# A decoder trunk in one kernel: PSUM in two halves with four lasting banks, and the up projection's first weight sums made beside the attention's output tiles

## The chip, the cores and the metric

The kernel runs on one core of a Trainium2 chip. The metric is the device time of one execution in microseconds (us), the median over several runs. One run is also profiled: its trace gives the start and length of every instruction on the engines: PE (TensorE, matmuls; PEld its weight loads), DVE (VectorE), ACT (ScalarE), POOL (GpSimd) and SP (SyncE, which issues most DMAs).

## The reference

Two decoder layers on x of 1024 positions x 1024 channels, all float32. Layer 0 mixes tokens with an RG-LRU block, layer 1 with RWKV-7 time mixing; both have a cross-attention into 256 memory positions and an MLP.

```python
for i in range(DEPTH):                       # DEPTH = 2
    g = ln_gains[i]
    hn = rms_norm(x, g[0])
    t = rglru_mixer(hn, ...) if i % 2 == 0 else rwkv7_mixer(hn, ...)
    x = x + rms_norm(t, g[1])
    c = mem_cross_attention(rms_norm(x, g[2]), mem_n, c_w_q[i], c_w_kv[i], c_w_o[i])
    x = x + rms_norm(c, g[3])
    m = sqrelu_mlp(rms_norm(x, g[4]), m_w_up[i], m_w_down[i])   # 1024 -> 4096 -> 1024
    x = x + rms_norm(m, g[5])
```

## The kernel before

**Products.** Every float32 operand of a large matmul is split into a high and a low part (`split`: the cast to the high part on ACT at L203, the subtraction that leaves the low part on DVE at L204), and `mm3` multiplies high x high, high x low and low x high (L304, L305, L306). One product of 128x128 weights with 512 columns is so three matmuls.

**PSUM.** Its 16 KB in each partition are eight banks of 512 float32. `psum_layout(two, one)` closes all pools and opens new ones: `two` pairs of banks (`psum()`, 128x1024, called p) and `one` single banks (`bank()`, 128x512, called q). The layouts are (4, 0) from the start and after the scan of the rwkv, (0, 8) in both MLPs and in the scan, (2, 4) in the rest of the rwkv. Since a new layout lies over the old one, the first tile of a new pool waits for the last reader of the old tiles that lay there.

**Phases.** `fphase` makes the transposed result of a projection, one weight tile of 128 columns into one pair of banks; it takes the weight tiles two by two. The queries of the cross-attention (`c_w_q`) have eight such tiles. `tphase` makes the untransposed result, one pair for each of the eight tiles of 128 positions (48 matmuls), and hands it to `post`, which `tail` gives: a root-mean-square of the tile (`rstd`: the square with its sum on ACT at L313, then two small POOL operations at L315 and L317), the gain (L611) and the residual (L612) on DVE, a second `rstd` for the next norm, and its scaling (L619). After four tiles the half is transposed on PE, by `transpose_in` (L345, with ACT at L348 and L350 and DVE at L354) or, ahead of the MLP, by `combine_in` (L370, ACT at L371).

**Cross-attention.** `xattn` runs the queries, then eight steps (four heads x two halves) of `scores`, `flip` (transposes of the softmax, L878) and `values`, each on a pair of banks, in a staggered order, and then the output projection, a `tphase` over `c_w_o`.

**MLP.** The up projection (`cphase`) multiplies 2x2 blocks with seven products rather than eight (p1 to p7), for 16 weight tiles of 256 columns. The sums of the activations (t1 to t4) come from `combine_in`, those of the weights (s1 to s4) from `combine_w`: four POOL operations of 128x512 (L412 once and L411 three times), three casts and three subtractions. `begin(i)` takes a weight tile, opens two banks and runs the first two products; `finish(i)` calls `combine_w`; then come p5, p6, p7, p3 and p4. The first two tiles go together: both `begin` and `finish`, then the transposes of the second half (`catch_up`), then each step for both. ACT copies and DVE additions take the results out (L453, L455, L464 to L486). Results are squared and spilled to DRAM with their sums; the down projection reads them back, again with seven products, and adds its banks into SBUF (L974, L976).

**Order.** The tile framework schedules the instructions: each engine runs its own list in order, and semaphores make one wait for another. The order on each list is decided when the kernel is built, so a change in buffers can reorder rows. `take` loads weights ahead of use on SP's queue; `depth` and `ahead` say how many.

**The rwkv's scan** goes through 16 chunks of 64 positions. Each chunk takes ten single banks in turn from the pool of eight.

Of the kernel before, what the change touches and what calls it, by code (L numbers as in the profile page):

```python
# [25 lines left out]
ROOM = {"w": 2}  # L26
D = 1024
KT = 8
# [19 lines left out]
class Net:  # L48
    def __init__(self, ctx, tc, I, plan=None):
# [4 lines left out]
        self.later, self.between = [], []  # L54
        self.depth, self.ahead = 2, 3
# [11 lines left out]
        self.pstack = None  # L67
        self.psum_layout(4, 0)
# [48 lines left out]
    def psum_layout(self, two, one):  # L117

        if self.rec:
            self.pp = self.pq = Nothing()  # L120
            return
        if self.pstack is not None:
            self.pstack.close()
        self.pstack = self.ctx.enter_context(ExitStack())
        pool = lambda n, b: self.pstack.enter_context(self.tc.tile_pool(name=self.nm(n), bufs=b, space=PSUM))
        self.pp = pool("pp", two) if two else None
        self.pq = pool("pq", one) if one else None
# [4 lines left out]
    def bank(self):  # L132
        return self.pq.tile([128, 512], F32, name=self.nm("q"), tag="q")
# [149 lines left out]
    def part(self):  # L283

        return self.bank() if self.pq is not None else self.psum()[:, 0:512]

    def halves(self):

        if self.pq is not None:
            return [self.bank() for _ in range(2)]  # L290
        p = self.psum()
        return [p[:, 0:512], p[:, 512:1024]]
# [148 lines left out]
    def cphase(self, w, n, B, func, evac, ahead=2):  # L441
# [4 lines left out]

        def begin(i):
            two, first = self.take(("w", w, i))
            h, l = first
            x, z = self.part(), self.part()  # L450
# [4 lines left out]
            nc.vector.tensor_add(c0[:, a], c0[:, a], z)  # L455
            st[i] = x, c0, c1, two, first

        def finish(i):
            x, c0, c1, two, first = st[i]
            st[i] = x, [], c0, c1, self.combine_w(two, first)  # L460

        def p6(x, y, c0, c1, A):
            self.product(x, A["s2"], B["t2"], False, False)
            nc.scalar.copy(c0[:, b], x)  # L464

        def p5(x, y, c0, c1, A):
            y.append(self.part())
            self.product(y[0], A["s1"], B["t1"], True, False)
            nc.scalar.copy(c1[:, b], y[0])

        def p7(x, y, c0, c1, A):
            self.product(x, A["s3"], B["t3"], False, False)
            nc.vector.tensor_add(c1[:, b], c1[:, b], x)

        def p3(x, y, c0, c1, A):
# [3 lines left out]
        def p4(x, y, c0, c1, A):  # L479
# [17 lines left out]
        def together(two, mid=lambda: None):  # L497
# [7 lines left out]
            for step in (p5, p6, p7, p3, p4):  # L505
                for i in two:
                    step(*st[i])
# [3 lines left out]
        together(range(ahead), self.catch_up)  # L511
        for i in range(ahead, n - 2):
# [3 lines left out]
            for step in (p6, p5, p7, p3, p4):  # L516
                step(*st[i])
# [27 lines left out]
    def tphase(self, rows, z, post):  # L545
# [10 lines left out]
        for tt in range(8):  # L556
# [9 lines left out]
            post(tt, p)  # L566

# [100 lines left out]
    def rglru(self, xt, post):  # L668
# [85 lines left out]

        w = I["a_w_out"][0]
# [78 lines left out]
    def xattn(self, layer, xt, post):  # L834
# [39 lines left out]
        def flip(e):  # L874
            p = self.psum()
            for mt in range(2):
                for i in range(4):
                    nc.tensor.transpose(p[:, mt * 512 + i * 128:mt * 512 + i * 128 + 128],  # L878
                                        e[:, i * 256 + mt * 128:i * 256 + mt * 128 + 128], self.ident)
            return self.split(p)  # L880

        def values(hd, hf, pt):
            ph, pl = pt
            p = self.psum()
            for j in range(2):
                c = slice(hd * 256 + j * 128, hd * 256 + j * 128 + 128)
                for mt in range(2):
                    s = slice(mt * 512, mt * 512 + 512)
                    vh, vl = vt[mt]
                    self.mm3(p[:, j * 512:j * 512 + 512], (vh[:, c], vl[:, c]), (ph[:, s], pl[:, s]), mt == 0, mt == 1)  # L890
            nc.scalar.copy(z[hf][:, 2 * hd:2 * hd + 2, :], p.rearrange("p (j t) -> p j t", t=512))
# [11 lines left out]
        self.tphase([w[k * 128:k * 128 + 128, :] for k in range(KT)], self.tile_of(z), post)  # L903


    def mlp(self, layer, xt, raw, post, late=None):
# [30 lines left out]
        self.psum_layout(0, 8)  # L937
        rest = self.cphase(up, 16, xt, AF.Relu, out)
        self.depth, self.ahead = DOWN
# [11 lines left out]
        W = lambda g: self.take(("d", down[g * 1024:g * 1024 + 1024, :], g))  # L951
        W(0)
        for g in range(4):
# [3 lines left out]
            for n, (name, qa, qb, bank, begins, ends, to) in enumerate(steps):  # L957
                if n == 5 and g < 3:
                    W(g + 1)
                A = self.take(("a", g, qa))  # L960
                B = self.take(("b", qb, g))
                for p in range(4):
                    if begins:
                        ps[bank, p] = self.bank()
# [138 lines left out]
def rwkv(self, X, xt, lw_wa, lw_g, post):  # L1103
# [13 lines left out]
    self.psum_layout(2, 4)  # L1117
# [369 lines left out]
    def scan_gram(c, groups):  # L1487
# [3 lines left out]
        for g in groups:  # L1491
            gt = self.unit()[:, 0:768].rearrange("p (q h w) -> p q h w", q=2, h=2)
            pv = self.bank().rearrange("p (q h w) -> p q h w", q=2, h=2)
# [11 lines left out]
            if c < 15:  # L1505
                if g % 2 == 0:
                    s["tp"] = self.bank().rearrange("p (q h i) -> p q h i", q=4, h=2)
# [33 lines left out]
    def flip_out(c):  # L1541
        s = cst.pop(c)
        y, (g1, g2) = s["y"], s["gs"]
        p = self.part()
# [23 lines left out]
    self.psum_layout(0, 8)  # L1568
    for h in range(2):
        nc.gpsimd.memset(cst[0]["sv"][hr[h], :, h, :], 0.0)  # L1570
    for c in range(16):
# [10 lines left out]
        yp = self.bank()  # L1582
        Y = yp.rearrange("p (q i) -> p q i", i=64)
        for m in range(2):
            ph = self.bank()
# [46 lines left out]
    self.psum_layout(4, 0)  # L1632
# [10 lines left out]
def network(net, I, out):  # L1643
# [12 lines left out]
    for l in range(2):  # L1656
# [5 lines left out]
        net.xattn(l, nxt, post)  # L1662
# [27 lines left out]
```

## Time and profile before

| | us |
|---|---|
| median of 3 runs | 3017.53 (3016.5 to 3020.7) |
| profiled execution, its own time | 3011.39 |
| its span in the trace | 3009.7 |
| PE busy | 2867.0 |
| DVE busy | 1811.5 |
| ACT busy | 1357.9 |
| POOL busy | 1152.8 |

A busy time is the sum of an engine's instructions; engines run beside each other, so the five don't add up to the span. The views quoted below are: the page (shares of the span), the waits of an engine (for whom it stood idle, how long in total, how often, and the longest), windows (busy times in one stretch of the span, with the clock that TensorE was granted, 1.00 being full speed), and the timeline (start, length, engine, line, operation, tiles out<-in, shape, count; in brackets the idle time before it and what ended that).

### The profile page before, as it was taken

How to read it: one execution, taken by the hardware profiler on the slowest of the kernel's cores; microseconds unless marked ns; L12 is line 12 of the kernel's file. 1: busy time of each engine (PE TensorE's matmuls, PEld its weight loads, DVE VectorE, ACT ScalarE, POOL GpSimd, SP SyncE). 2: the span in 40 equal slices, each digit the busy share in tenths (PEclk: the TensorE clock that was granted, in tenths of full speed). 3: DMA queues.
4: the chain of work that ended last, by engine and by line, in shares of the span. 5: the costliest groups of instructions: out<-in, count | busy, mean ns of one | idle time of the engine just before them, and what ended most of it. 6: DMA issues, size and time to landing. Idle time of an engine off the chain costs nothing. (4 is left out here: it accounts for less than half of the span.)

```text
span 3009.7 us, 42878 instructions
## 1 busy us (share of the span) xinstructions
PE 2867.0 (95%) x16987; PEld 2382.3 (79%) x16987; DVE 1811.5 (60%) x1996; ACT 1357.9 (45%) x1943; POOL 1152.8 (38%) x1055
## 2 busy tenths in 40 slices
PE   7999999898999999989999899989999899999998
PEld 6888798786888878877877578878888688887886
DVE  5576552547345688867785536884354744568776
ACT  6464342535455543347442534442243545454332
POOL 2000100015666664431486225651001556667442
PEclk9999999998999999999999999999999999999999
DMA  8213261122444564332656889852312244455443
GB/s 258 73 46 94 88 210 60 57 84 70 153 154 152 213 225 146 119 116 89 183 155 183 220 246 228 175 127 96 100 50 77 84 140 154 154 210 203 158 136 119
DMA packets 382889, 421.93 MB, mean 140 GB/s; under 512 B 91248, under 2 KB 293216, under 8 KB 382688
## 3 DMA queue, kind: packets, MB, share of 16 engines
q1 hardware_dynamic: 370656, 379.19, 42.0%
q0 software_dynamic: 11568, 39.41, 3.5%
q8 instruction: 134, 2.20, 0.3%
q14 instruction: 67, 0.55, 0.1%
q10 hardware_dynamic: 464, 0.59, 0.1%
HBM read 284.31 MB, written 134.74 MB: 139 GB/s over the span
## 5 line engine op out<-in xcount | busy, mean ns | idle before, releaser
L204 DVE TENSOR_TENSOR u<-u,u 128x1024 fp32r<-128x1024 f32 (+1 forms) x518 | 818.6, 1608 | 355.3 <-ACT u L203 335.3
L304 PE MATMUL p<-u,u 128*128 128x512 f32 (+1 forms) x1920 | 716.7, 376 | 18.2 <-ACT u L203 9.5
L203 ACT CAST u<-u 128x1024 fp32r<-128x1024 f32 (+1 forms) x550 | 542.7, 1024 | 421.4 <-PE q L305 158.7
L305 PE MATMUL p<-u,u 128*128 128x512 f32 (+1 forms) x1920 | 718.1, 374 | 9.4 <-DVE u L204 9.4
L306 PE MATMUL p<-u,u 128*128 128x512 f32 (+1 forms) x1920 | 714.9, 373 | 3.8 <-DVE u L204 3.7
L304 PE MATMUL q<-u,u 128*128 128x512 f32 (+1 forms) x1632 | 642.5, 395 | 25.2 <-ACT u L203 8.3
L305 PE MATMUL q<-u,u 128*128 128x512 f32 (+1 forms) x1632 | 638.5, 392 | 7.0 <-DVE u L204 7.0
L306 PE MATMUL q<-u,u 128*128 128x512 f32 (+1 forms) x1632 | 633.6, 391 | 0.0
L304 PEld LDWEIGHTS p<-u,u 128*128 128x128 f32 x1920 | 366.5, 191 | 84.5 <-ACT u L203 13.5
L305 PEld LDWEIGHTS p<-u,u 128*128 128x128 f32 x1920 | 367.6, 191 | 74.5 <-DVE u L204 14.6
L306 PEld LDWEIGHTS p<-u,u 128*128 128x128 f32 x1920 | 367.2, 191 | 67.4 <-DVE u L204 5.8
L315 POOL TENSOR_SCALAR s<-s 128x1 f32<-128x1 f32 x98 | 36.1, 369 | 992.2 <-ACT u L313 991.2
L304 PEld LDWEIGHTS q<-u,u 128*128 128x128 f32 (+1 forms) x1632 | 308.3, 190 | 97.0 <-ACT u L203 13.5
L305 PEld LDWEIGHTS q<-u,u 128*128 128x128 f32 (+1 forms) x1632 | 308.8, 189 | 73.0 <-DVE u L204 9.3
L306 PEld LDWEIGHTS q<-u,u 128*128 128x128 f32 (+1 forms) x1632 | 308.3, 189 | 64.4
L431 POOL TENSOR_TENSOR u<-u,u 128x1024 f32<-128x1024 f32 x64 | 179.2, 2823 | 86.5 <-DVE u L204 80.4
L976 DVE TENSOR_TENSOR z<-z,q 128x512 f32<-128x512 f32 x192 | 128.9, 681 | 90.4 <-PE q L306 90.2
L204 POOL TENSOR_TENSOR u<-u,u 128x1024 fp32r<-128x1024 f32 x32 | 95.0, 2968 | 164.0 <-ACT u L203 101.9
L411 POOL TENSOR_TENSOR u<-u,u 128x512 f32<-128x512 f32 x96 | 150.8, 1580 | 2.9
L927 POOL TENSOR_TENSOR u<-u,u 128x512 f32<-128x512 f32 x32 | 47.1, 1471 | 166.2 <-ACT u L916 160.1
L304 PE MATMUL q<-z,u 128*128 128x512 f32 x256 | 102.1, 399 | 7.0 <-DVE u L611 7.0
L611 DVE SCALAR_TENSOR_TENSOR u<-p,s,u 128x1024 f32<-128x1024 f32 x24 | 30.8, 1284 | 122.1 <-ACT u L203 77.9
(260 smaller groups left out, 3536.5 us busy)
## 6 DMA issues: line engine op xcount, KB each, us to landing
u<-d SPq DMA_DIRECT2D x198, 512.0 KB, 4.4
d<-u SPq DMA_DIRECT2D x109, 512.0 KB, 3.5
d<-u POOLq DMA_DIRECT2D x68, 512.0 KB, 4.1
d<-u SPq DMA_DIRECT2D x132, 256.0 KB, 3.7
u<-in_m_w_up SPq DMA_DIRECT2D x64, 512.0 KB, 5.8
u<-in_m_w_down SPq DMA_DIRECT2D x64, 512.0 KB, 5.9
u<-in_c_w_kv SPq DMA_DIRECT2D x32, 512.0 KB, 6.5
u<-d SPq DMA_DIRECT2D x56, 256.0 KB, 6.1
```

Of the source, the lines that this page charges most:

```text
L203: self.nc.scalar.copy(hv, src)
L204: (eng or self.nc.vector).tensor_tensor(lv, src, hv, ALU.subtract)
L304: mm(o, ah, bh, start=first, stop=False, **kw)
L305: mm(o, ah, bl, start=False, stop=False, **kw)
L306: mm(o, al, bh, start=False, stop=last, **kw)
L315: nc.gpsimd.tensor_scalar(v, ss, 1.0 / n, eps, ALU.mult, ALU.add)
L411: sub = lambda o, x, y: nc.gpsimd.tensor_tensor(o, x, y, ALU.subtract)
L431: self.nc.gpsimd.tensor_tensor(f[o][i], f[x][i], f[y][i], ALU.subtract)
L611: nc.vector.scalar_tensor_tensor(o, src, r, gb, ALU.mult, ALU.mult)
L927: tt(s1, r21, r22, ALU.add)
L976: nc.vector.tensor_add(to_, to_, o)
```

## The change

PSUM is seen as two halves of four banks. The first, `still`, is opened once, at the first output projection (`a_w_out`), and its four single banks are kept to the end of the kernel. The other half is either two pairs ("mixed") or four more single banks ("banks"). Until `a_w_out` all eight banks are four pairs ("pairs"), as before. `bank(n)` takes pool n modulo the number of single pools.

- In the layout "mixed" (output projections, queries, cross-attention, rwkv but for its scan) there are two pairs where there were four; the transposes, the memory's keys and values, `flip` and `values` use still banks, with a split or a copy for each half.
- `fphase` takes its first two weight tiles together and each further one alone.
- `make` takes up the weight tiles 0 and 1 of the up projection, and makes their sums (`combine_w`), after tiles 5 and 6 of the attention's output projection (`MAKE`); `begin` and `finish` use what is there.
- In `cphase` the first two tiles stand in still banks (`place`), and the layout "banks" is opened after the transposes of the second half; from then on tiles alternate between the two pools.
- `then` takes up the first weights and operands of the down projection behind p7 of the last two tiles, where they were taken after the up projection.
- The scan chooses its banks by chunk, group or half.

Core of the diff:

```diff
-    def psum_layout(self, two, one):
+    def psum_layout(self, kind):
...
+        if self.stack_a is not None:
+            self.stack_a.close()
+        if kind != "pairs" and self.stack_b is None:
+            self.stack_b = self.ctx.enter_context(ExitStack())
+            self.still = pool(self.stack_b, 4)
+        self.stack_a = self.ctx.enter_context(ExitStack())
+        other = pool(self.stack_a, {"pairs": 4, "mixed": 2, "banks": 4}[kind])
+        self.pp = None if kind == "banks" else other
+        self.pqs = [] if kind == "pairs" else [self.still] if kind == "mixed" else [self.still, other]
...
+    def bank(self, n=0):
...
+        return self.pqs[n % len(self.pqs)].tile([128, 512], F32, name=self.nm("q"), tag="q")
...
+MAKE = (5, 6)
+    def make(self, w, i):
+        self.depth, self.ahead = 0, 2 - 2 * i
+        two, first = self.take(("w", w, i))
+        self.made[i] = two, first, self.combine_w(two, first)
...
+        place = lambda i: 0 if i < ahead else (i + 1) % 2
...
+            x, z = self.bank(place(i)), self.bank(place(i))
...
+                if step is p7 and two[-1] == n - 1:
+                    with self.behind():
+                        then()
...
+        def second_half():
+            self.catch_up()
+            self.psum_layout("banks")
+        together(range(ahead), second_half)
...
-        for i in range(0, len(fs), 2):
-            pair = fs[i:i + 2]
+        for pair in [fs[:2]] + [[f] for f in fs[2:]]:
...
             post(tt, p)
+            if mid:
+                mid(tt)
...
-    self.psum_layout(2, 4)
+    self.psum_layout("mixed")
...
-    self.psum_layout(0, 8)
+    self.psum_layout("banks")
...
-        net.xattn(l, nxt, post)
+        net.xattn(l, nxt, post, lambda tt: tt in MAKE and net.make(I["m_w_up"][l], MAKE.index(tt)))
```

What that does to the lists of the engines, at three places. In the rows an operation stands with its tiles out<-in; s are small tiles of statistics, u and z tiles in SBUF, p pairs and q single banks in PSUM. The lines of the new kernel are some 14 to 33 higher: L203 is L217, L313 is L327, L315 and L317 are L329 and L331, L411 and L412 are L425 and L426, L453 is L476, L304 to L306 are L318 to L320.

POOL at the end of layer 0's output projection, before: the statistics of the last tile, then the sums of weight tile 0 (u_4621 and u_4622) and the first of tile 1.

```order
L315 TENSOR_SCALAR s_5244<-s_5242 128x1
L317 TENSOR_TENSOR s_5246<-s_5244,nhalf 128x1
L315 TENSOR_SCALAR s_5255<-s_5253 128x1
L317 TENSOR_TENSOR s_5257<-s_5255,nhalf 128x1
L315 TENSOR_SCALAR s_5265<-s_5263 128x1
L317 TENSOR_TENSOR s_5267<-s_5265,nhalf 128x1
L412 TENSOR_TENSOR u_5319<-u_4622 128x512
L411 TENSOR_TENSOR u_5320<-u_4621,u_4622 128x512
L411 TENSOR_TENSOR u_5319<-u_5319,u_4621 128x512
L411 TENSOR_TENSOR u_5320<-u_4621,u_5319 128x512
L412 TENSOR_TENSOR u_5374<-u_4634 128x512
```

And in the new kernel, where u_4688 and u_4689 are weight tile 1:

```order
L329 TENSOR_SCALAR s_5252<-s_5250 128x1
L331 TENSOR_TENSOR s_5254<-s_5252,nhalf 128x1
L426 TENSOR_TENSOR u_5272<-u_4689 128x512
L425 TENSOR_TENSOR u_5273<-u_4688,u_4689 128x512
L425 TENSOR_TENSOR u_5272<-u_5272,u_4688 128x512
L329 TENSOR_SCALAR s_5263<-s_5261 128x1
L425 TENSOR_TENSOR u_5273<-u_4688,u_5272 128x512
L331 TENSOR_TENSOR s_5265<-s_5263,nhalf 128x1
L329 TENSOR_SCALAR s_5341<-s_5339 128x1
L331 TENSOR_TENSOR s_5343<-s_5341,nhalf 128x1
L329 TENSOR_SCALAR s_5352<-s_5350 128x1
L331 TENSOR_TENSOR s_5354<-s_5352,nhalf 128x1
```

The sums of weight tile 1 now stand between the statistics of the last three tiles, and those of tile 0 further ahead; behind the last statistics no weight sum is left.

ACT at the same place, before: p_5192 is the pair of the output projection's last tile, q_5289 the first bank of the up projection.

```order
L313 ACTIVATE u_5241,s_5242<-p_5192 128x1024
L313 ACTIVATE u_5173,s_5253<-u_5180 128x1024
L203 CAST u_5285<-u_4633 128x1024
L313 ACTIVATE u_5241,s_5263<-u_5248 128x1024
L453 COPY u_5291<-q_5289 128x512
L203 CAST u_5325<-u_5319 128x1024
L203 CAST u_5329<-u_5320 128x1024
L203 CAST u_5333<-u_4622 128x512
L203 CAST u_5340<-u_5281 128x1024
L453 COPY u_5346<-q_5344 128x512
L203 CAST u_5380<-u_5374 128x1024
```

And in the new kernel, where these are p_5289 and q_5374:

```order
L327 ACTIVATE u_5102,s_5261<-u_5109 128x1024
L217 CAST z_5244<-u_5226 128x1024
L217 CAST u_5278<-u_5272 128x1024
L217 CAST u_5282<-u_5273 128x1024
L217 CAST u_5286<-u_4689 128x512
L327 ACTIVATE u_5338,s_5339<-p_5289 128x1024
L476 COPY u_5376<-q_5374 128x512
L327 ACTIVATE u_5249,s_5350<-u_5256 128x1024
L327 ACTIVATE u_5338,s_5360<-u_5345 128x1024
L476 COPY u_5406<-q_5404 128x512
```

The casts of weight tile 1's sums (u_5272, u_5273 and u_4689) went from behind the first bank's copy to a place ahead of the last tile's square.

PE in layer 0's queries, before: p_3529 and p_3530 are the pairs of the first two weight tiles, p_3707 that of the third.

```order
L305 MATMUL p_3707<-u_2837,u_3519 128x512
L306 MATMUL p_3707<-u_2833,u_3520 128x512
L304 MATMUL p_3707<-u_2833,u_3519 128x512
L304 MATMUL p_3529<-u_3582,u_3445 128x512
L304 MATMUL p_3530<-u_3582,u_3475 128x512
L305 MATMUL p_3707<-u_2837,u_3519 128x512
L306 MATMUL p_3707<-u_2833,u_3520 128x512
L305 MATMUL p_3529<-u_3586,u_3445 128x512
L306 MATMUL p_3529<-u_3582,u_3446 128x512
L305 MATMUL p_3530<-u_3586,u_3475 128x512
```

And in the new kernel, where the first two are p_3540 and p_3541 and the third p_3716:

```order
L318 MATMUL p_3541<-u_3593,u_3486 128x512
L319 MATMUL p_3540<-u_3597,u_3456 128x512
L320 MATMUL p_3540<-u_3593,u_3457 128x512
L319 MATMUL p_3541<-u_3597,u_3486 128x512
L320 MATMUL p_3541<-u_3593,u_3487 128x512
L318 MATMUL p_3716<-u_2839,u_3530 128x512
L319 MATMUL p_3716<-u_2843,u_3530 128x512
L320 MATMUL p_3716<-u_2839,u_3531 128x512
```

Before, matmuls of the third tile stood among the last of the first two, in a pair that was free; now the third begins when both are through.

More of the change, by code (lines that the diff above doesn't have):

```diff
@@ L115, in small, with pool @@
         return self.sp.tile([128, 4], F32, name=self.nm("s"), tag="s")[:, :n]
-    def psum_layout(self, two, one):
+    def psum_layout(self, kind):
         if self.rec:
-            self.pp = self.pq = Nothing()
+            self.pp, self.pqs = Nothing(), []
             return
[L122 to L127, printed above, removed]
+        def pool(stack, bufs):
+            return stack.enter_context(self.tc.tile_pool(name=self.nm("pm"), bufs=bufs, space=PSUM))
+        if self.stack_a is not None:
[7 more added lines that the diff above has]
+        self.pqs = [] if kind == "pairs" else [self.still] if kind == "mixed" else [self.still, other]
     def psum(self):
         return self.pp.tile([128, 1024], F32, name=self.nm("p"), tag="p")
-    def bank(self):
-        return self.pq.tile([128, 512], F32, name=self.nm("q"), tag="q")
+    def bank(self, n=0):
+        if self.rec:
+            return Nothing()
+        return self.pqs[n % len(self.pqs)].tile([128, 512], F32, name=self.nm("q"), tag="q")
     def dram(self, shape, dt=F32):
@@ L283, in part @@
     def part(self):
-        return self.bank() if self.pq is not None else self.psum()[:, 0:512]
+        return self.bank() if self.pqs else self.psum()[:, 0:512]
     def halves(self):
-        if self.pq is not None:
-            return [self.bank() for _ in range(2)]
+        if self.pqs:
+            return [self.bank(n) for n in range(2)]
         p = self.psum()
@@ L445, in cphase @@
         st = {}
+        place = lambda i: 0 if i < ahead else (i + 1) % 2
         def begin(i):
-            two, first = self.take(("w", w, i))
+            two, first = self.made[i][:2] if i in self.made else self.take(("w", w, i))
             h, l = first
-            x, z = self.part(), self.part()
+            x, z = self.bank(place(i)), self.bank(place(i))
             c0, c1 = self.unit(), self.unit()
@@ L506, in together @@
                 for i in two:
-                    step(*st[i])
+                    step(*st[i], i)
+                if step is p7 and two[-1] == n - 1:
+                    with self.behind():
+                        then()
             for i in two:
                 end(i)
-        together(range(ahead), self.catch_up)
+        def second_half():
+            self.catch_up()
+            self.psum_layout("banks")
+        together(range(ahead), second_half)
         for i in range(ahead, n - 2):
@@ L936, in mlp, with then @@
         self.depth, self.ahead = UP
-        self.psum_layout(0, 8)
-        rest = self.cphase(up, 16, xt, AF.Relu, out)
-        self.depth, self.ahead = DOWN
+        W = lambda g: self.take(("d", down[g * 1024:g * 1024 + 1024, :], g))
+        ops = []
+        def then():
+            self.depth, self.ahead = 0, 0
+            W(0)
+            ops.extend([self.take(("a", 0, 0)), self.take(("b", "b11", 0))])
+            self.depth, self.ahead = DOWN
+        rest = self.cphase(up, 16, xt, AF.Relu, out, then)
         acc = self.big((4, 1024))
@@ L1543, in flip_out @@
         y, (g1, g2) = s["y"], s["gs"]
-        p = self.part()
+        p = self.bank(c + 1)
         for q in range(4):
```

65 lines of the change are left out of this document (32 added, 33 removed).

## The prediction

> **What bounds the kernel now.** The page first: the share of the span by engine.
>
> ```profile
> span 3009.7 us, 42878 instructions
> PE 2867.0 (95%) x16987; PEld 2382.3 (79%) x16987; DVE 1811.5 (60%) x1996; ACT 1357.9 (45%) x1943; POOL 1152.8 (38%) x1055
> ```
>
> PE is busy in 95% of the span and no other engine is over 60%. The change alters no matmul's size and adds none, so it can pay only in what PE loses: idle time between matmuls, and matmuls at a lower granted clock. Second, the windows view, for the stages that the diff touches (length, busy time of PE, PEld, DVE, ACT and POOL, granted clock, DMA share, GB/s):
>
> ```profile
> 692.70:763.20 70.50, 56.00 (x225) 44.64 (x226) 52.55 (x36) 39.42 (x52) 37.63 (x23) 0.85 0.25 73
> 2355.30:2425.80 70.50, 55.80 (x226) 44.56 (x226) 52.64 (x36) 39.42 (x52) 37.80 (x23) 0.85 0.25 74
> 760.00:1090.00 330.00, 329.06 (x1452) 271.83 (x1451) 180.90 (x132) 171.22 (x216) 224.26 (x163) 1.00 0.54 183
> 1840.00:2010.00 170.00, 158.55 (x2830) 141.87 (x2831) 141.34 (x345) 78.59 (x214) 109.46 (x132) 1.00 0.82 179
> ```
>
> The body of the first MLP (third row) has nothing to win: 1452 matmuls in 330.0 us, 0.227 us each, PE idle for 0.9 us. The starts of both MLPs (first two rows) are poor: 192 matmuls and 32 transposes take 70.5 us, of which 14.5 are idle, at a clock of 0.85. The scan (last row) has 11.5 us of idle in 170. Third, the waits view of PE (who waits, for what, us in total, times, longest):
>
> ```profile
> PE q L304 <- ACT u L203: 8.3, 4, 2.5
> PE q L304 <- DVE u L611: 7.0, 2, 3.5
> PE q L304 <- ACT z L350: 6.6, 1, 6.6
> PE q L304 <- ACT u L464: 6.1, 2, 3.0
> PE q L1625 <- DVE u L1611: 5.2, 9, 2.9
> PE q L370 <- DVE u L455: 4.7, 2, 2.4
> PE q L1589 <- DVE u L1619: 4.5, 7, 1.5
> PE q L370 <- ACT u L371: 3.4, 2, 1.8
> ```
>
> A wait of L304 on L611 is no want of data: L611 is the last reader of the output projection's last pair of banks, and the MLP's pool of eight banks opens over that pair. L350 is the same at the rwkv's entry. These two waits are what the still banks can remove.
>
> **MLP starts, two of them.** T is 692.69, where the output projection's last matmul ends. PE's rows after it:
>
> ```profile
> 696.18 0.50 PE L304 MATMUL q<-z,u 128*128 128x512 f32 x1 [3.50 <-DVE u L611]
> 713.52 0.93 PE L370 MATMUL q<-ident,u 128*128 128x128 f32 x4 [2.35 <-DVE u L455]
> 716.23 1.97 PE L370 MATMUL q<-ident,u 128*128 128x128 f32 x8 [1.79 <-ACT u L371]
> 745.45 0.79 PE L304 MATMUL q<-u,u 128*128 128x512 f32 x1 [3.04 <-ACT u L464]
> ```
>
> The 3.50 us are the wait for the last pair; the first 48 matmuls then run largely at half clock (0.50 us and more each). The 2.35 us before the transposes come from DVE, and DVE is late because of POOL. The three engines beside it:
>
> ```profile
> 692.78 1.02 ACT L313 ACTIVATE u<-p 128x1024 f32<-128x1024 f32 x1 [1.96 <-PE p L306]
> 698.02 1.06 ACT L313 ACTIVATE u<-u 128x1024 f32<-128x1024 f32 x1 [2.15 <-DVE u L612]
> 715.50 4.15 ACT L371 ACTIVATE u<-q,colt 128x512 f32<-128x512 f32 x7
> ...
> 697.84 1.22 DVE L204 TENSOR_TENSOR u<-u,u 128x1024 fp32r<-128x1024 f32 x1
> 700.12 1.76 DVE L619 TENSOR_SCALAR u<-u,s 128x1024 f32<-128x1024 f32 x1 [1.06 <-POOL s L317]
> 705.40 7.46 DVE L204 TENSOR_TENSOR u<-u,u 128x1024 fp32r<-128x1024 f32 x4 [1.07 <-ACT u L203]
> 720.61 5.30 DVE L204 TENSOR_TENSOR u<-u,u 128x1024 fp32r<-128x1024 f32 x2 [1.41 <-ACT u L203]
> 728.23 18.95 DVE L204 TENSOR_TENSOR u<-u,u 128x1024 fp32r<-128x1024 f32 x9
> ...
> 700.05 1.28 POOL L412 TENSOR_TENSOR u<-u 128x512 f32<-128x512 f32 x1
> 705.62 2.28 POOL L412 TENSOR_TENSOR u<-u 128x512 f32<-128x512 f32 x1
> 707.86 6.13 POOL L411 TENSOR_TENSOR u<-u,u 128x512 f32<-128x512 f32 x3
> ```
>
> The sums of weight tiles 0 and 1 (eight POOL operations, L411 and L412) run from T+7.4 to T+21.3, between the moment when PE could go on and the transposes. The change moves them, their six casts and six subtractions beside projection tiles 6 and 7, where each tile keeps PE busy for 48 x 0.227 = 10.9 us. New schedule, step by step:
> - The first 48 matmuls start at T, since the four still banks aren't held by the projection: 10.9 us, to T+10.9.
> - The transposes need tile 7's last operation (L619), which ends at T+9.2 now (700.12 + 1.76). In the new order of ACT the three casts of the second combination stand ahead of tile 7's statistics (some 2.6 us by the casts' usual 1.05, 1.05 and 0.5), so I take T+12: a gap of about 1 us.
> - Of the four still banks two hold the first products, so the 32 transposes run through two. A group of four takes 0.98 on PE and 0.59 on ACT (4.15 / 7); two banks give (0.98 + 0.59) / 2 = 0.79 a group, and eight groups 6.3: T+18.5 to T+19.
> - The 10 products p5 to p4 of both tiles are 120 matmuls, 27.2 us. DVE sets the pace as before: its splits of t1 took 2.65 each (5.30 / 2), the nine that follow 2.1. From the end of the transposes t1 is there after 7.7, t2 after 14.2, and from p7 on PE is behind: about 33 us with some 5.5 idle, to T+52. Now part of the third tile's first products fills these waits (PE takes them out of turn); in the new order it stands behind p4, so the holes are bare.
> - The third tile's 24 matmuls: 5.4, T+57.5. With 1 to 3.5 us for a clock that falls in those holes: T+58.5 to T+61.
>
> Against T+70.5 that is 9.5 to 12 for each MLP; I take 10.5 each, **21 in all**. The bounds: 3 each if POOL comes late (a rival below), 14 if the holes close as well.
>
> What hides the moved work: POOL, ACT and DVE beside tiles 6 and 7. The eight POOL operations cost 1.28 each alone and up to 2.28 beside DVE, so 10 to 18 us in 21.8 us of two tiles, where POOL otherwise does only the statistics. Queued behind them on POOL are just those statistics (L315, L317): for tile 6 there is a whole tile of slack, for tile 7 none. The two weight tiles are loaded long before, so SP's queue gains nothing there.
>
> How the two engines get on beside each other: a DVE split takes 1.22 alone and 7.46 / 4 = 1.87 or 5.30 / 2 = 2.65 beside POOL, a POOL sum 1.28 or 2.28. [...]
>
> **Queries (c_w_q), two of them.** Before, four pairs of banks serve weight tiles two by two, the next two free. Now there are two pairs: both are in use by the first two tiles, whose matmuls alternate and end together, so the third tile waits for an evacuation. No such wait is in the trace; the rows nearest to it:
>
> ```profile
> 536.83 1.01 ACT L203 CAST u<-p 128x1024 fp32r<-128x1024 f32 x1 [4.42 <-PE p L306]
> 537.87 1.23 DVE L204 TENSOR_TENSOR u<-p,u 128x1024 fp32r<-128x1024 f32 x1 [4.21 <-ACT u L203]
> 1571.42 0.47 PE L304 MATMUL p<-u,u 128*128 128x512 f32 x1 [1.94 <-DVE u L1354]
> 1539.65 0.64 PE L304 MATMUL p<-u,u 128*128 128x512 f32 x1 [2.79 <-DVE u L1185]
> ```
>
> Cast and subtraction of one pair take 2.3 us after its last matmul, so PE idles about 2.0; after 1.94 the next matmul still took 0.47 and after 2.79 it took 0.64, so a stretch at half clock may follow (1.7 us if 3.4 us long). Bounds 2.0 and 3.7 each, I take 2.9: **5.8 lost**. The later single tiles cover their 2.3 us with 10.9 us of matmuls.
>
> **The core of the cross-attention.** Two pairs serve the scores alone, the flips and values get single banks with a copy for each half, which frees them sooner, at two more operations for each step on ACT. I take +0.75 for each layer, **1.5** (-1 to +3).
>
> **Entry of the rwkv.**
>
> ```profile
> 1346.29 0.80 PE L304 MATMUL q<-u,u 128*128 128x512 f32 x1 [6.59 <-ACT z L350]
> 1365.19 0.75 DVE L619 TENSOR_SCALAR u<-u,s 128x1024 f32<-128x1024 f32 x1 [0.72 <-POOL s L317]
> 1370.91 1.91 PE L345 MATMUL q<-ident,u 128*128 128x128 f32 x16
> ```
>
> The 6.59 go: the still banks carry over. But the next transposes (1370.91) need L619 of the last tile, which ends at 1365.95 whatever PE does. PE saves at most 1370.91 - 1365.95 = **4.9** (0 to 9, the top if DVE moves up too); the rest turns into a wait on L619.
>
> **At nothing:** the scan's banks by number (-4 to +4; its matmuls keep their order) and the earlier first weights of the down projection (-3 to +3; layer 0's border between up and down lies inside the third row of the windows, where PE idles 0.9 us in all).
>
> **Sum:** 21 - 5.8 + 1.5 + 4.9 = 21.6. The profiled execution took 3011.4 (span 3009.7 and 1.7 around it); 21.6 less is 2989.8. The median of the runs, 3017.5, lies 6.1 over that execution, so **2996**.
>
> **The rivals.**
> - *POOL is late.* If contention stretches the eight sums past T, tile 7's statistics stand behind them, and the transposes start at T+16 and not T+12, with a stretch at half clock on top: 5 to 6 less at each MLP. With 3.7 lost at each query phase the gain is near 9: 3009. For: DVE rows that double beside POOL. Against: 21.8 us of cover. 17%.
> - *It doesn't do what it says.* The still banks are also those of the first half's transposes (L370); if these are held, the first matmuls wait as before. Gain: -5.8 + 1.5 + 4.9, about 0.6: 3017. For: four banks, eight transposes' groups. Against: those end during tile 7. 8%.
> - *The shorter waits cost no clock.* The wait of 1.94 left the next matmul at 0.47. If the waits that are left (all under 3 us) lower no clock, 0.9 at each query phase and some 2 at each MLP come back: about 6, 2990. Against: matmuls of 0.64 after 2.79 and of 0.79 after 3.04 (745.45). 10%. [...]
> - *Slower: the scan.* Its banks came from one ring of eight; now from two rings of four, chosen by chunk and group. If a chunk's bank is still read when its number comes round, PE waits there in each of 16 chunks. To turn 21.6 into a loss of 6 it takes 27.6 / 16 = 1.7 us a chunk: 3025 at 1.8 us. For: the waits L1589 and L1625 show a chain with no slack. Against: a chunk takes ten banks (one for y, two for the maps, six for the next chunk's products, one for the flip), so a ring of four comes round in most of a chunk, not in a step. 5%.
>
> **How the numbers follow.** The forecast has 60%, from 2985 to 3005. The range goes from 2979 (the MLP starts at their upper bound) to 3012 (the late POOL with its unknowns). 0.2%, 6 us, is about what a measurement can tell: faster 83% (the forecast, the clock rival, three quarters of the late POOL), within 12%, slower 5%.
>
> **What would show it.** Right: at both MLP starts the first matmul within 0.3 us of the projection's last; transposes at about T+12; 192 matmuls by T+61; no L350 wait at the rwkv but one on L619; a new wait of about 2 us in each c_w_q; the scan's row unchanged within 4 us. Wrong: projection tiles 6 and 7 over 10.9 us each, tile 7's L317 behind L411's successor after T+3, or waits on reused banks in the scan.

## The result, and the profile after

| | before | after |
|---|---|---|
| median of the runs, us | 3017.0 (4 runs) | 2990.6 (4 runs) |
| ratio after to before | | 0.9916, 95% interval 0.9904 to 0.9928 |
| span of the profiled execution, us | 3009.7 | 2990.2 |

The change makes the kernel 0.8% faster, 22 to 29 us by the interval and 19.5 us by the two profiled executions. The forecast was 2996, in a range from 2979 to 3012. The page after, the same two lines as before:

```profile
span 2990.2 us, 42725 instructions
PE 2861.3 (96%) x16987; PEld 2381.1 (80%) x16987; DVE 1812.9 (61%) x2012; ACT 1355.9 (45%) x1975; POOL 1166.1 (39%) x1055
```

PE is busy for 5.7 us less with the same number of recorded instructions (its mean granted clock is 0.983 where it was 0.980), and idle for less. The windows of the two MLP starts and of the first MLP's body after the change (length, busy time of PE, PEld, DVE, ACT, POOL, granted clock, DMA share, GB/s):

```profile
690.80:750.30 59.50, 52.64 (x226) 41.35 (x225) 41.96 (x33) 36.73 (x49) 30.59 (x20) 0.94 0.35 115
...
760.00:1075.00 315.00, 313.63 (x1379) 258.10 (x1378) 172.02 (x126) 163.40 (x208) 211.12 (x152) 1.00 0.54 181
```

The first row is the work of the row of 70.50 us before, 192 matmuls and 32 transposes: 59.5 us now, 6.9 of them idle in place of 14.5, at a clock of 0.94 in place of 0.85. PE's waits after:

```profile
PE q L318 <- DVE z L1014: 8.2, 3, 3.9
...
PE q L359 <- ACT u L1171: 4.4, 1, 4.4
...
PE q L384 <- DVE u L650: 3.5, 2, 1.7
```

The waits for L611 (7.0 us), for L350 (6.6), for L464 (6.1) and of the transposes for L455 (4.7) are gone or small. In their place stand a wait of the second half's transposes for the last tile's scaling (L650, which was L619), one at the rwkv's entry, and two long ones in the down projections (L1014, which was L976).

The span cut at points that both traces have: the first scores of each cross-attention, the end of its output projection (T), the 192nd matmul of the up projection after T, and the start of the last addition of the down projection. Times are in us.

| stretch | before | after | saved | forecast |
|---|---|---|---|---|
| start to layer 0's first scores | 538.8 | 540.9 | -2.0 | -2.9 |
| layer 0: cross-attention to T | 153.9 | 150.0 | 3.9 | 0.8 |
| layer 0: T to 192 matmuls | 70.6 | 59.5 | 11.1 | 10.5 |
| layer 0: rest of the MLP | 576.1 | 582.8 | -6.7 | 0 |
| rwkv and layer 1's queries | 863.8 | 859.2 | 4.6 | 4.9 - 2.9 |
| layer 1: cross-attention to T | 152.2 | 149.3 | 2.9 | 0.7 |
| layer 1: T to 192 matmuls | 70.6 | 60.3 | 10.3 | 10.5 |
| layer 1: rest of the MLP | 573.5 | 578.8 | -5.3 | 0 |
| the end | 10.3 | 9.5 | 0.8 | 0 |
| all | 3009.7 | 2990.2 | 19.5 | 21.6 |

The sum came out within 2.1 us, but two terms that were nearly nothing in the forecast are not: the rest of the MLPs lost 12 us, and the cross-attentions gained 5 more than forecast. The experiments take these apart.

### The profile page after: what moved, and what is told of

Same layout as the page of the kernel before. It is cut to its first block, busy times and chain, and to the rows that moved or that the text cites. A ratio compares the mean times of both kernels' runs of the same rounds, so it can differ in the third digit from the quotient of the medians.

```text
span 2990.2 us, 42725 instructions
## 1 busy us (share of the span) xinstructions
PE 2861.3 (96%) x16987; PEld 2381.1 (80%) x16987; DVE 1812.9 (61%) x2012; ACT 1355.9 (45%) x1975; POOL 1166.1 (39%) x1055
## 5 line engine op out<-in xcount | busy, mean ns | idle before, releaser
L217 ACT CAST u<-u 128x1024 fp32r<-128x1024 f32 (+1 forms) x550 | 542.8, 1023 | 372.7 <-PE q L319 139.6
L319 PE MATMUL q<-u,u 128*128 128x512 f32 (+2 forms) x1824 | 699.8, 385 | 12.4 <-DVE u L218 12.1
L318 PE MATMUL q<-u,u 128*128 128x512 f32 (+2 forms) x1824 | 696.6, 386 | 12.9 <-DVE z L1014 8.2
L320 PE MATMUL q<-u,u 128*128 128x512 f32 (+2 forms) x1824 | 694.3, 384 | 1.1 <-DVE u L218 1.1
L318 PE MATMUL p<-u,u 128*128 128x512 f32 (+1 forms) x1728 | 658.6, 384 | 22.7 <-ACT u L217 9.7
L319 PE MATMUL p<-u,u 128*128 128x512 f32 (+1 forms) x1728 | 657.1, 380 | 6.2 <-DVE u L218 6.2
L320 PE MATMUL p<-u,u 128*128 128x512 f32 (+1 forms) x1728 | 656.2, 380 | 3.5 <-DVE u L218 3.5
L329 POOL TENSOR_SCALAR s<-s 128x1 f32<-128x1 f32 x98 | 38.1, 389 | 969.0 <-ACT u L327 949.6
L318 PEld LDWEIGHTS q<-u,u 128*128 128x128 f32 (+1 forms) x1824 | 344.4, 189 | 84.7 <-DVE z L1014 8.8
L319 PEld LDWEIGHTS q<-u,u 128*128 128x128 f32 (+1 forms) x1824 | 344.7, 189 | 82.7 <-DVE u L218 16.2
L318 PEld LDWEIGHTS p<-u,u 128*128 128x128 f32 x1728 | 331.6, 192 | 87.8 <-ACT u L217 14.7
L320 PEld LDWEIGHTS q<-u,u 128*128 128x128 f32 (+1 forms) x1824 | 344.6, 189 | 69.0 <-DVE u L218 2.2
L319 PEld LDWEIGHTS p<-u,u 128*128 128x128 f32 x1728 | 331.8, 192 | 66.8 <-DVE u L218 10.5
L320 PEld LDWEIGHTS p<-u,u 128*128 128x128 f32 x1728 | 331.3, 192 | 65.7 <-DVE u L218 5.2
L1014 DVE TENSOR_TENSOR z<-z,q 128x512 f32<-128x512 f32 x192 | 129.0, 680 | 84.8 <-PE q L320 84.2
L425 POOL TENSOR_TENSOR u<-u,u 128x512 f32<-128x512 f32 x96 | 152.7, 1596 | 3.1
L320 PE MATMUL q<-z,u 128*128 128x512 f32 x256 | 99.5, 390 | 1.1 <-DVE u L218 1.1
```

Of the source, the lines that this page charges most:

```text
L217: self.nc.scalar.copy(hv, src)
L318: mm(o, ah, bh, start=first, stop=False, **kw)
L319: mm(o, ah, bl, start=False, stop=False, **kw)
L320: mm(o, al, bh, start=False, stop=last, **kw)
L329: nc.gpsimd.tensor_scalar(v, ss, 1.0 / n, eps, ALU.mult, ALU.add)
L425: sub = lambda o, x, y: nc.gpsimd.tensor_tensor(o, x, y, ALU.subtract)
```

## The experiments

Ratios are to the kernel before, run on the same chip; small effects are read from the spans of the profiled executions (2990.2 for the changed kernel) and from their stretches. Single executions of the changed kernel differ by up to 7 us, so a difference of a few us between two spans counts only where a stretch shows it too.

### What the lasting banks and the weight sums do at the MLP's start

**The lasting banks without the sums.**

```diff
-MAKE = (5, 6)
+MAKE = ()
```

> The changed kernel with no weight sums ahead of the MLP (its two tiles' sums are made at the MLP's start, as before the change); the lasting banks stay. Theory (both parts count): the first matmul still follows the output projection at once, but the transposes wait for the sums again, so each MLP start takes about 7 us more than in the changed kernel (T+66 to T+68 for its first 192 matmuls against T+59.5); 14 us over the changed kernel, about 3005. Rival (the lasting banks do it all): within 3 us of the changed kernel, about 2991.

Ratio 0.9953 (0.9940 to 0.9965), span 2996.6. PE at layer 0's start, and POOL after T = 690.8:

```profile
700.27 0.50 PE L320 MATMUL q<-z,u 128*128 128x512 f32 x1 [3.12 <-DVE u L218]
711.68 6.62 PE L384 MATMUL q<-ident,u 128*128 128x128 f32 x28 [4.54 <-DVE u L478]
...
693.94 1.28 POOL L426 TENSOR_TENSOR u<-u 128x512 f32<-128x512 f32 x1
...
704.33 5.62 POOL L425 TENSOR_TENSOR u<-u,u 128x512 f32<-128x512 f32 x3
```

The first matmul follows T at once, but the sums run from T+3.1 to T+19, tile 1's first split comes late (3.12) and most transposes start at T+20.9. The 192 matmuls end at T+63.3 and T+63.0: 3.8 and 2.7 us later than in the changed kernel, not 7. Both parts count, but the sums only for half of what I expected, since PE has the first products to do while they run.

**The sums without the lasting banks:** the kernel before with `make` and its two callers added.

```diff
-    def tphase(self, rows, z, post):
+    def tphase(self, rows, z, post, mid=None):
...
             post(tt, p)
+            if mid:
+                mid(tt)
```

> The kernel before, with its PSUM layouts, and only the weight sums moved beside output tiles 5 and 6. Theory (both parts count, and add): the first matmul waits 3.5 us for the last pair as before, the transposes no longer wait for POOL, and each MLP start is 6 to 8 us shorter: 12 to 16 under the kernel before, about 3003. Rival (the two work only together): under 4 us gained.

Ratio 0.9976 (0.9967 to 0.9985), span 3004.9. PE and POOL at layer 0's start, T = 694.6:

```profile
701.78 0.80 PE L306 MATMUL q<-z,u 128*128 128x512 f32 x1 [7.21 <-DVE u L621]
...
692.66 1.05 POOL L317 TENSOR_SCALAR s<-s 128x1 f32<-128x1 f32 x1
693.78 2.13 POOL L413 TENSOR_TENSOR u<-u,u 128x512 f32<-128x512 f32 x1
695.87 1.53 POOL L319 TENSOR_TENSOR s<-s,nhalf 128x1 f32<-128x1 f32 x1
698.61 0.23 POOL L317 TENSOR_SCALAR s<-s 128x1 f32<-128x1 f32 x1 [1.21 <-ACT u L315]
698.92 1.41 POOL L319 TENSOR_TENSOR s<-s,nhalf 128x1 f32<-128x1 f32 x1
```

The transposes start at T+20.3 and run without a wait, but the wait for the last pair (L621, L611 in the kernel before) has doubled, from 3.50 to 7.21: the casts and the last sum stand ahead of tile 7's statistics, and the eight banks of the MLP open over its pair. The 192 matmuls end at T+64.7 and T+64.5. So the four cases, in us from T (layer 0, layer 1):

| | sums at the MLP's start | sums beside the output tiles |
|---|---|---|
| PSUM as before | 70.6, 70.6 | 64.7, 64.5 |
| lasting banks | 63.3, 63.0 | 59.5, 60.3 |

The banks alone give 7.4, the sums alone 6.0, both 10.7. They don't add up fully.

**The place of the sums.**

```diff
-MAKE = (5, 6)
+MAKE = (6, 7)
```

> The changed kernel with the sums after output tiles 6 and 7 instead of 5 and 6. Theory (POOL's lateness decides, by way of tile 7's statistics): tile 1's sums stand beside tile 7's statistics after T, the transposes start some 4 us later than T+13.6, and each MLP start is 3 to 5 us longer: 6 to 10 over the changed kernel, about 2999. Rival (the cover is ample, the place of the sums does not matter): within 2 us of the changed kernel.

Ratio 0.9952 (0.9939 to 0.9966), span 2996.8: 6.6 over the changed kernel. PE at the transposes, T = 691.0:

```profile
708.38 3.52 PE L384 MATMUL q<-ident,u 128*128 128x128 f32 x16 [4.38 <-DVE u L478]
```

The transposes start at T+17.4, the 192 matmuls end at T+63.3 and T+64.1. One tile too late costs as much as leaving the sums where they were. And one tile earlier:

```diff
-MAKE = (5, 6)
+MAKE = (4, 5)
```

> The changed kernel with the sums after output tiles 4 and 5, one tile earlier. Theory (tile 7's statistics wait for POOL's last sum, which ends 3 us after T): with the sums gone by T the transposes start at about T+12 and not T+13.6, 1 to 2 us less at each MLP start, 2 to 4 under the changed kernel. Rival (the sums' six more SBUF tiles, held one tile longer, or the earlier casts and subtractions delay the output tiles): the output projection's tiles take over 10.9 us each, and the kernel is slower than the changed one.

Ratio 0.9896 (0.9880 to 0.9913), span 2980.4. The row of PE where the transposes start, T = 689.2, beside those of the changed kernel, T = 690.8:

```profile
700.90 1.09 PE L384 MATMUL q<-ident,u 128*128 128x128 f32 x8 [0.41 <-DVE u L478]
```

```profile
702.17 0.55 PE L384 MATMUL q<-ident,u 128*128 128x128 f32 x3 [0.47 <-DVE u L478]
704.46 4.00 PE L384 MATMUL q<-ident,u 128*128 128x128 f32 x17 [1.73 <-DVE u L650]
```

With the sums one tile earlier all transposes run from T+10.7 to T+16.7, and the 192 matmuls end at T+56.2 in both layers, 3.3 and 4.1 us sooner. The wait for L650 is gone. ACT shows how POOL held tile 7 up in the changed kernel: two casts of tile 1's sums, which wait for POOL's last sum, stand ahead of the square of tile 7.

```profile
693.95 1.57 ACT L217 CAST u<-u 128x1024 fp32r<-128x1024 f32 x2 [2.31 <-POOL u L425]
695.42 1.02 ACT L327 ACTIVATE u<-p 128x1024 f32<-128x1024 f32 x1
```

The square so starts at T+4.6; with the sums one tile earlier it starts at T. The rival of the late POOL was real, at 3 to 4 us an MLP rather than 5 to 6; of the 2.9 us at the transposes' start the forecast had priced 1.3 (T+12 against T+10.7).

### The start of the down projection

The first down weights and operands taken up after the up projection, as before the change:

```diff
-        rest = self.cphase(up, 16, xt, AF.Relu, out, then)
+        rest = self.cphase(up, 16, xt, AF.Relu, out, lambda: None)
+        self.depth, self.ahead = DOWN
...
+        W(0)
         for g in range(4):
```

> The changed kernel with the first down weights and operands taken up after the up projection, as before the change. Theory (taking them up early is what costs 3 to 5 us at the start of each down projection): the wait of 3.9 us at the second group of the down projection goes back to 2.5, with no stretch at half clock, 5 to 9 us under the changed kernel, about 2984. Rival 1 (the wait comes from POOL and DVE splitting the second group's operands, whenever the first is taken): within 2 us of the changed kernel. Rival 2 (the early take-up pays): over the changed kernel by 3 or more.

Ratio 0.9889 (0.9875 to 0.9902), span 2979.7. PE's wait ahead of the down projection's second group, in the changed kernel and in this one, with DVE beside it:

```profile
1091.59 0.80 PE L318 MATMUL q<-u,u 128*128 128x512 f32 x1 [3.88 <-DVE z L1014]
...
1081.26 9.68 DVE L218 TENSOR_TENSOR u<-u,u 128x1024 fp32r<-128x1024 f32 x3
1090.86 0.67 DVE L1014 TENSOR_TENSOR z<-z,q 128x512 f32<-128x512 f32 x1
```

```profile
1081.25 0.47 PE L318 MATMUL q<-u,u 128*128 128x512 f32 x1 [2.31 <-DVE z L1009]
...
1071.01 9.49 DVE L218 TENSOR_TENSOR u<-u,u 128x1024 fp32r<-128x1024 f32 x3
1080.43 0.67 DVE L1009 TENSOR_TENSOR z<-z,q 128x512 f32<-128x512 f32 x1
```

In both, three splits of 3.2 us each stand ahead of the addition that PE waits for, so the splits alone don't make the difference; what differs is their place on DVE's list: behind the eighth addition of the down projection here, behind the eleventh in the changed kernel. Without the early take-up the wait is 2.31, near the 2.46 of the kernel before, and the next matmul takes 0.47, not 0.80. The rest of the MLP takes 578.6 and 574.6 us, against 582.8 and 578.8: 4.2 us in each layer are the price of the early take-up, 1.6 of it the longer wait and most of the rest the clock (in layer 0 it was 0.50 from 1090.03 to 1096.86 in the changed kernel, and 1.00 from 1078 to 1086 in this one). All eight profiled kernels with the operands taken up early take 582.2 to 582.9 and 578.0 to 580.1 us there, the three without 577.7 to 578.6 and 574.6 to 574.7. (The other 2 us of the span saved lie in the rwkv.) The next run tells which part of it:

```diff
             W(0)
-            ops.extend([self.take(("a", 0, 0)), self.take(("b", "b11", 0))])
```

> The changed kernel in which only the first down weights are taken up beside the last up tiles, and the first operands (with their splits) after the up projection. Theory (the early splits shift the order on DVE, so that the second group's wait grows from 2.3 to 3.9 us): the wait goes back to about 2.3 and the kernel is 5 to 10 us under the changed kernel, like the one without any early take-up. Rival (the early loads of the weights shift it): the 3.9 us stay, within 3 us of the changed kernel.

Ratio 0.9883 (0.9869 to 0.9896), span 2976.4. The wait is 2.85 us, with the clock at 1.00 after it (1084.7 to 1091.5), and the rest of the MLP takes 578.6 and 574.7 us, as without any early take-up. So the loads do no harm; taking up the operands, with their splits, does. That it acts by the order on DVE is read from these rows and not shown by itself. The span is 13.8 us under the changed kernel, over the 5 to 10 that I expected: besides the 8.3 us here, 3.7 lie in layer 1's cross-attention and MLP start, which this edit doesn't reach.

### The queries, one by one

```diff
-        for pair in [fs[:2]] + [[f] for f in fs[2:]]:
+        for pair in [[f] for f in fs]:
```

> The changed kernel with all eight weight tiles of the queries taken one by one, the first two as well. Theory (two pairs that end together cost a wait of 2 us and sometimes a stretch at half clock): the wait of 1.91 us before the third tile goes, 2 to 3.6 us at each of two places, 4 to 7 under the changed kernel, about 2985. Rival (the second tile's first half covers the transposes of the input's second half): without its 24 matmuls, 5.4 us, PE waits for those transposes, up to 5 us at each place, up to 10 over the changed kernel.

Ratio 0.9860 (0.9847 to 0.9874), span 2966.7: 23.5 us under the changed kernel, far over what I expected, so the gain had to be elsewhere. Layer 0's scores begin 3.4 us earlier, and its wait of 1.91 is gone; in layer 1 the same wait stays (1.91 us, before the third tile): the first two tiles seem to take turns there all the same. Some 20 us lie in the rwkv: the wait of 11.39 us ahead of L1435 is gone, and with it 13.65 us at half clock (1673.71 to 1687.36), 4.87 of which PE was busy (from 1655 to 1668, the place in this run, its matmuls take 0.39). ACT there, in the changed kernel and in this one:

```profile
1680.36 1.04 ACT L217 CAST u<-u 128x1024 fp32r<-128x1024 f32 x1 [11.99 <-DMA u<-in_b_w_rkv]
1681.42 1.01 ACT L1425 COPY u<-p 128x1024 f32<-128x1024 f32 x1
```

```profile
1659.69 1.04 ACT L217 CAST u<-u 128x1024 fp32r<-128x1024 f32 x1
1662.30 1.02 ACT L1425 COPY u<-p 128x1024 f32<-128x1024 f32 x1 [1.57 <-PE p L320]
```

In the changed kernel a cast that waits 12 us for a weight's load stands on ACT ahead of the copy that PE waits for. With single tiles the copy doesn't stand behind such a cast. Two runs test this reading: the single tiles in the queries alone, and in the kernel before everywhere but in the queries.

```diff
-        for pair in [fs[:2]] + [[f] for f in fs[2:]]:
+        for pair in [[f] for f in fs] if len(fs) == 8 else [fs]:
```

> The changed kernel with the eight weight tiles of the queries taken one by one, but the pairs of tiles in the rwkv's projections kept. Theory (the gain of some 20 us with single tiles everywhere comes from the rwkv, where a cast that waits for a late weight stands ahead of the copy that frees PE): only the 2.9 us of layer 0's queries are gained, nothing in layer 1, and the wait of 11.4 us in the rwkv stays: 2 to 4 us under the changed kernel. Rival (the queries' order moves the rwkv's loads): most of 23 us is gained here too.

Ratio 0.9908 (0.9895 to 0.9922), span 2986.1, 4.1 under the changed kernel; the wait in the rwkv is there, 11.79 us.

```diff
-        for i in range(0, len(fs), 2):
-            pair = fs[i:i + 2]
+        n = 1 if len(fs) == 2 else 2
+        for i in range(0, len(fs), n):
+            pair = fs[i:i + n]
```

> The kernel before with only the lists of two weight tiles taken one by one (the rwkv's and the recurrent block's projections); its queries still go in pairs. Theory (the 12.4 us wait of the rwkv and its stretch at half clock come from the pairs, whatever the layout of PSUM): 15 to 22 us under the kernel before, a ratio near 0.994. Rival (it takes the new layout, with its two pairs, to gain): within 5 us of the kernel before.

Ratio 0.9940 (0.9927 to 0.9954), span 2992.4, 17.3 under the kernel before (20.0 in the rwkv itself): those 17 to 20 us can be had without the change.

### The rwkv's entry and its scan

Pools closed and opened anew at the entry, and one ring of eight banks for the scan:

```diff
-    self.psum_layout("mixed")
+    self.psum_layout("new")
```

> The changed kernel with the lasting banks closed and opened anew at the rwkv's entry. Theory (the lasting banks earn 3.8 us there): the wait of 6.6 us for the transposes' last reader is back, and the stage takes 3 to 5 us more than in the changed kernel. Rival (the wait of 4.45 us that took its place gives all of it back): within 1 us.

Ratio 0.9932 (0.9918 to 0.9946), span 2993.6. From the start of the down projection's last addition to ACT's first copy of the scan's products it takes 483.8 us, against 480.0 with the lasting banks: 3.8 us. The row of PE with new pools, and the one that stands in its place in the changed kernel:

```profile
1340.05 0.80 PE L321 MATMUL q<-u,u 128*128 128x512 f32 x1 [6.22 <-DVE u L371]
```

```profile
1360.45 5.38 PE L359 MATMUL q<-ident,u 128*128 128x128 f32 x24 [4.45 <-ACT u L1171]
```

```diff
-    self.psum_layout("banks")
+    self.psum_layout("ring")
```

> The changed kernel with one ring of eight banks in the rwkv's scan, as before the change, in place of two pools of four chosen by chunk and group. Theory (the split of the banks costs nothing): the scan's 16 chunks take the same time within 2 us. Rival: the two pools cost or earn over 3 us in the scan.

Ratio 0.9921 (0.9908 to 0.9934), span 2989.4: no difference that can be told. Within the rwkv the ring reaches that first copy 5.2 us earlier and takes 7.7 us more from there to the scan's last (188.0, against 180.3 in the changed kernel and 184.5 in the kernel before), so that the two together are 2.5 us over the changed kernel's. So the theory of equal times doesn't hold for the chunks by themselves: there the two pools earn more than 3 us, as the rival says. Most of it is lost again ahead of the scan, and the span doesn't show the rest.

### The two edits that were faster, together

Single tiles everywhere, and the first down weights and operands taken up after the up projection.

> The changed kernel with the two edits that were each faster: all weight tiles of the projections taken one by one, and the first down weights taken up after the up projection. Theory (the two work at different places, the queries and the rwkv's projections on one side, the start of the down projections on the other): the savings add, 23.5 + 10.5 = 34 us under the changed kernel in the profiled executions, a ratio of 0.980 to 0.984 to the kernel before. Rival (part of each was the same chance of the clock): a ratio over 0.985.

Ratio 0.9825 (0.9812 to 0.9839), span 2958.7: 31.5 us under the changed kernel, 51.0 under the one before. The savings add nearly in full. Whether the sums after tiles 4 and 5 would add to this was not tried.

## Why the prediction was right

**The MLP starts** (forecast 10.5 each, measured 11.1 and 10.3) came out by the steps that were given. The first matmul follows T without a wait (L611's 3.50 us gone); three transposes start at T+11.3 and the rest at T+13.6 (forecast T+12); they end at T+20.0 (T+18.5 to T+19); the 192 matmuls are done at T+59.5 (T+58.5 to T+61). The step that was late is tile 7's chain. The forecast put three casts, 2.6 us, ahead of tile 7's square; what held it up were the two casts shown above, which began only when POOL's last sum had ended, 3.1 us after T. POOL's rows:

```profile
684.97 0.19 POOL L329 TENSOR_SCALAR s<-s 128x1 f32<-128x1 f32 x1 [12.91 <-ACT u L327]
...
691.76 2.15 POOL L425 TENSOR_TENSOR u<-u,u 128x512 f32<-128x512 f32 x1
693.87 1.53 POOL L331 TENSOR_TENSOR s<-s,nhalf 128x1 f32<-128x1 f32 x1
696.61 0.23 POOL L329 TENSOR_SCALAR s<-s 128x1 f32<-128x1 f32 x1 [1.21 <-ACT u L327]
696.93 1.41 POOL L331 TENSOR_TENSOR s<-s,nhalf 128x1 f32<-128x1 f32 x1
```

The cover of 21.8 us was long enough: POOL stood idle for 12.91 of it. But tile 1's sums stand behind tile 6's first statistics on POOL's list, and the square for these started 7.4 us after tile 6's last matmul (683.76 and 676.36), behind the copies and casts of the first half's transposes on ACT. The sums had only the last 5.1 us before T left. It is the place on the lists that I didn't follow, not the sum of the durations; the run with the sums one tile earlier gains 3.3 and 4.1 us by it. In these rows POOL was slower beside DVE's splits: the last sum took 2.15 us and not 1.28, the small operation behind it 1.53 and not 0.55. Tile 7's three DVE operations took 1.27, 1.21 and 0.75 us, all after the last sum. That the transposes came 1.6 us after the forecast comes from the queue on ACT. One reading of mine was wrong from the start: in the kernel before, the first 48 matmuls did not run largely at half clock; the clock was back at 1.00 at 700.11, after 10 of them as the trace counts.

**The queries** (forecast 2.9 lost each, bounds 2.0 and 3.7): the wait is 1.91 us in both layers, and in both 3.41 us at half clock follow (from 472.22 and from 2124.27), which makes some 3.6 us each by estimate (1.91 and half of 3.41), near the upper bound. Taking the tiles one by one brings back 3.4 to 4.4 us in layer 0. Right; the table's loss of 2.0 in the first stretch is smaller, so something else there gains, which was not taken apart.

**The cross-attentions** (forecast 0.75 each) saved 3.9 and 2.9. This term was too small. Shorter waits are part of it (in layer 0 the waits from the first scores to T sum to 7.6 us before and 6.5 after, in layer 1 to 7.1 and 4.7). The clock is another: at half clock stood 6.83 us of this stretch before and 3.41 after in layer 0, but 3.41 before and 6.83 after in layer 1, so that it helps by some 1.7 us (half of 3.41, an estimate) in the one and costs as much in the other. No part of the change explains that (the last section shows where such drops stood). What the halves of `flip` and `values` do by themselves was not tried, so the shares stay open.

**The rwkv's entry** (forecast 4.9): 3.8 by the run with new pools. The wait of 6.59 us went, and the transposes' wait for the last tile's scaling took its place as forecast: L650 ends at 1360.10, the transposes start at 1360.45. The row names L1171: the first of two copies there ended at 1360.40, 0.3 us after L650. In the table this stretch is 4.6 better, of which the new wait in layer 1's queries takes back some 3.6; about 4 us must lie elsewhere in the rwkv. The scan's chunks are 4.2 us shorter than before, which would cover it; that was not tested.

**The border from up to down** (forecast nothing, bounds 3 either way) is the step that failed. I put the early take-up at nothing because PE didn't idle at the border. It doesn't now either. The price shows some 75 us later, where PE waits for DVE, 4.2 us in each layer. The window that I read ended at 1090.00; the kernel before already waited there, 2.46 us from 1091.05 on, so there was a wait to lengthen. Of the 6.7 us lost in layer 0, the other 2.5 are mostly a stretch at half clock (3.41 us from 1318.73) after a later wait of 2.46 us, 2.05 before; the run without the early take-up still takes 578.6 us there, 2.5 over the kernel before.

**The scan** (forecast nothing, bounds 4 either way): its chunks take 4.2 us less than before, at the edge of the bounds; the slower rival, which priced it at 1.7 us a chunk, has no sign in the trace.

**The sum.** Against the profiled execution 21.6 were forecast and 19.5 came. The large term was right; that the others came out near their sum is luck, since their errors nearly cancel (in the table six stretches were 10 us better than forecast in all, three 12 us worse). On the runs the forecast of 2996 is 5.4 too high, because I carried over that the profiled execution before had been 6.1 below the median. That distance isn't the kernel's: after the change the profiled execution took 2991.9, 1.3 over the median. The lower end of the range, 2979, doesn't follow from the reason given for it: both MLP starts at their upper bound of 14 make 7 us more, which is 2989.

## What to carry to other kernels

A pool of buffers that opens over another makes its first user wait for the last reader of the old one (3.50 us ahead of the MLP here); a few buffers that stay across the border give the engine work there, and it pays most when the next thing that engine needs is late as well (7.4 us with the weight sums late, 4.7 with them early). Work that is moved into a cover must be through before the chain that ends the cover, not before the cover ends, and what counts is where it stands on each engine's list, not whether its durations fit: one output tile earlier was worth another 3 to 4 us for each MLP, one tile later lost all that the move had brought. And an engine that runs its list in order is to be read at the row ahead of the one that others wait for: a cast that waits 12 us for a load on ACT cost 17 to 20 us, more than the lasting banks brought at any one place.

## What the runs showed of the hardware

The granted clock fell after waits of about 2 us, and not by the wait's length alone. The kernel before waits 2.05 us until 538.84; the changed kernel waits 1.91 us until 471.63 and, at the place of the first, 2.05 us until 540.86. The windows view around these three (PE's busy time is the second number, the clock the third from the end):

```profile
536.28:539.69 3.41, 1.01 (x5) 0.39 (x3) 1.82 (x2) 2.86 (x4) 0.00 (x0) 1.00 0.00 0
539.69:543.10 3.41, 2.81 (x13) 2.81 (x14) 3.41 (x4) 1.93 (x3) 0.00 (x0) 0.50 0.01 2
```

```profile
468.81:472.22 3.41, 1.50 (x8) 0.91 (x7) 1.87 (x2) 2.87 (x3) 0.00 (x0) 1.00 0.46 154
472.22:475.63 3.41, 3.41 (x10) 2.64 (x9) 1.62 (x2) 0.00 (x0) 0.00 (x0) 0.50 0.02 5
...
537.08:540.49 3.41, 1.74 (x8) 1.12 (x6) 0.59 (x1) 1.64 (x2) 0.00 (x0) 1.00 0.00 0
540.49:543.90 3.41, 2.29 (x15) 1.96 (x16) 3.41 (x4) 3.16 (x4) 0.00 (x0) 1.00 0.00 0
```

The same wait of 2.05 us was followed by a drop in one kernel and by none in the other. The windows here are cut by a step that the traces show: within each of the two, all stretches at half clock begin at whole multiples of 3.413 us from one another (in the kernel before those at 539.69, 696.70 and 1816.27, for instance, are 46 and 374 of them apart from the first). A wait that lies in one window (2.40 us idle in the first row, 1.91 in the third) is followed by a window at half clock; the one that a border cuts (1.67 and 1.12 idle) is not. In these two traces, cut in this way from 30 us on, all 38 windows at full clock with over 1.7 us idle are followed by half clock, and of the 1637 with less only one. So in these traces a stretch of 3.41 us at half clock, some 1.7 us by estimate (half of it), came or didn't come after a wait of about 2 us with the place where the wait lay. The forecast had nothing that told this place, and each of its terms for the clock was uncertain by about as much.
